# Residual block, one core: SwiGLU results, residual blocks and most mixer outputs turned into tables by DMA transposes of 16-bit halves instead of TensorE transposes

## The chip, the cores and the metric

The kernel runs on one core of one Trainium2 chip. The metric is the device time of one execution in microseconds (us), the median of several runs. TensorE (PE) multiplies, VectorE (DVE) and ScalarE (ACT) work on tiles in SBUF and PSUM, GpSimd (POOL) does little here, and SyncE (SP) issues the DMAs of the weights.

## The reference

One layer of a streaming encoder on 256 tokens of width 2048, all in fp32:

```python
proj = rmsnorm(x, g_mix) @ w_in                  # 2048 x 10240: two mixers' q, k, v and two gates
merged = sigmoid(gate_sb) * (y_sb @ w_sb_out) + sigmoid(gate_ca) * (y_ca @ w_ca_out)
x = x + merged @ w_mix_out                       # 2048 x 2048
g_ff, u_ff = split(rmsnorm(x, g_ffn) @ w_ffn_in) # 2048 x 11264
x = x + (silu(g_ff) * u_ff) @ w_ffn_out          # 5632 x 2048
x = x + sigmoid(rmsnorm(x, g_ple) @ w_ple_gate) * (p @ w_ple_in)
out = rmsnorm(x, g_final)
```

`y_sb` and `y_ca` are two attention mixers of 8 heads each. With 256 tokens, nearly all the work is the products of the 256-row activations with the weights.

## The kernel before

**Tables.** A product needs its activations with the contracted feature on the partitions. They stand in *tables*: T1 (the input, later the merged mixer output, later the input of the last gate), T2 (the mixers' outputs, later the SwiGLU results) and T3 (the input of the feed-forward). A table holds for each of up to 16 feature tiles of 128 a high part and a low part (`fp32r` splits of the fp32 value); every product is made of three fp32r matmuls, high with high, high with low, low with high (`three`, L305).

**How a table is made.** `into_table` (L473) takes a 256-token by 512-feature fp32 block (`src`). TensorE transposes it in eight 128x128 transposes into PSUM (L482). `table_part` (L489) then makes the split: ScalarE copies PSUM to the high part (L504), VectorE subtracts for the low part (L505, by `minus`, L257). Where the feature pair is one that is multiplied by a fast scheme of seven products instead of eight (a "pair"), ScalarE copies PSUM to a plain tile `af` first (L496), and `sums_of` (L462) makes four sums (`fm`) and their split (the forms FP, F_more, F_out, F_last). For a norm's input each value is scaled by the gain on the way (L508, L509). 23 blocks become tables this way: 4 of the merged mixer output (key `mg`), 4 of the residual for the feed-forward (`ffn`), 11 of SwiGLU results (`h0`, `h1`, `h2`: 3, 4 and 4 blocks) and 4 of the residual for the last gate (`ple`).

**Weights.** They are streamed. SP issues one DMA of 512 KB for each raw tile (L241) into seven places (five, and two more in the late part of the kernel); it waits until a place has been read. ScalarE casts a raw tile to its high part `hi` (L277, and L292, L295 for the two tiles of a pair piece), VectorE subtracts to make `lo` (L257). Up to four `hi` and `lo` tiles exist, and TensorE multiplies from them.

**Order.** The work is a list of *pieces*. A single piece has one raw tile and twelve 512-wide matmuls; a pair piece has two raw tiles and 21 matmuls. `flush` (L436) loops over the pieces: it loads as far as there are places, splits up to three pieces ahead, and writes out the products of the present one. Other work is a queue of tasks, one of which is run after a piece; `later` puts a table's making three tasks behind. `split` (L259) runs tasks at once when a piece needs a table that isn't made yet. A scheduler then sets the order in each engine's queue, which is executed in that order.

The feed-forward takes 3 blocks of 12, 16 and 16 feature tiles. In each, 3 or 4 units make a SwiGLU block (two 512-wide weight columns, 16 raw tiles) and put it into C; then two units multiply with `w_ffn_out`. C is one buffer with four 512-wide slots, C[:, 0] to C[:, 3]: the result stands in the first two; the last two are free after `in_post` has used them. The pieces of the first output unit of the first block come in the order 0, 0, 1, 1, -2, 3, 3, -4, 5, 5 (L40; a minus is a pair piece), and piece -4 needs the forms F_more of the last SwiGLU block of that part.

Of the kernel before, what the change touches and what calls it, by code (L numbers as in the profile page):

```python
# [8 lines left out]

F32 = mybir.dt.float32  # L10
F32R = mybir.dt.float32r
AF = mybir.ActivationFunctionType
ALU = mybir.AluOpType
AX = mybir.AxisListType
# [2 lines left out]
P = 128  # L17
S = 256
# [34 lines left out]
def block_kernel(ctx: ExitStack, tc: tile.TileContext, x, p, w_in, w_sb_out, w_ca_out, w_mix_out,  # L53
# [95 lines left out]
    pieces = []  # L149
    held = deque()  # L150
    tasks = deque()
    done = set()

    def run_task():
# [104 lines left out]
    def split(pc):  # L259
        for k in pc["needs"]:  # L260
            while k not in done:
                run_task()
        raws = pc.pop("raw")
        state["raw"] -= len(raws)
        for _ in raws:
            held.popleft()
        if pc["g"]["kind"] == "unit" and len(raws) == 2:
            return split_pair(pc, *raws)
        raw, = raws
        n = raw.shape[1]  # L270
        if pc["g"]["keep"] is None:
            hi, lo = buffers(n)
        else:
            hi, lo = (t[:, pc["kts"][0] * pc["ncol"] :][:, :n] for t in pc["g"]["keep"])
        m = n // 2 if pc is pieces[0] else n
        for c in range(0, n, m):
            state["cast"] = nc.scalar.copy(hi[:, c : c + m], raw[:, c : c + m])  # L277
# [158 lines left out]
    def flush(every=1, until=None, in_turn=False):  # L436

        n = 0
        while state["at"] < len(pieces) and (until is None or until not in done):
            pc = pieces[state["at"]]  # L440
            prefetch()
            products(pc)
            seed_next()
            state["at"] += 1
            n += 1
            if tasks and every and not state["hold"] and int(n / every) > int((n - 1) / every):
# [39 lines left out]
        for k in range(4):  # L486
            done.add((key, 4 * c + k))

    def table_part(dst, kt, ps, gain, forms, pairs):  # L489
        n = ps.shape[1]  # L490
        ks = slice(kt, kt + n)
        g = None if gain is None else [gT[:, gain + kt + k : gain + kt + k + 1] for k in range(n)]
        if forms is not None and kt // 2 in pairs:
            af = state["work"]("af").rearrange("p (k s) -> p k s", k=2)
            if g is None:
                nc.scalar.copy(af, ps)  # L496
            else:
                for k in range(2):
                    nc.scalar.activation(af[:, k, :], ps[:, k, :], AF.Identity, scale=g[k])
            nc.scalar.copy(dst[:, ks, 0, :], af)  # L500
            minus(dst[:, ks, 1, :], af, dst.bitcast(F32)[:, ks, 0, :])
            sums_of(af, forms(kt))
        elif g is None:
            nc.scalar.copy(dst[:, ks, 0, :], ps)  # L504
            minus(dst[:, ks, 1, :], ps, dst.bitcast(F32)[:, ks, 0, :])  # L505
        else:
            for k in range(n):
                nc.scalar.activation(dst[:, kt + k, 0, :], ps[:, k, :], AF.Identity, scale=g[k])  # L508
                nc.vector.scalar_tensor_tensor(dst[:, kt + k, 1, :], ps[:, k, :], g[k], dst.bitcast(F32)[:, kt + k, 0, :],  # L509
                                               ALU.mult, ALU.subtract)  # L510
# [412 lines left out]
    def out_post(m, c):  # L923
        def post(ps):
            cs = slice(c * NB, (c + 1) * NB)
            gt = gates[:, :, m, cs]
            for t in range(NT):
                by = rstd if (m, c) == (1, 0) else r1
                with tc.issue_after(state["cast"].ins):
                    nc.scalar.activation(gt[:, t, :], gt[:, t, :], AF.Sigmoid, scale=by["mix"][:, t : t + 1])  # L930
            for t in range(NT):
                nc.vector.tensor_tensor(gates[:, t, m, cs], ps[t], gates[:, t, m, cs], ALU.mult)
            if m == 1:
                mg = gates[:, :, 0, cs]
                nc.vector.tensor_tensor(mg, mg, gt, ALU.add)
                later(lambda: into_table(T1, c, mg, key="mg", forms=lambda kt: FP[:, kt // 4 - 2], pairs=MIX_PAIRS))
        return post

    for m, wo in ((0, w_sb_out), (1, w_ca_out)):
# [27 lines left out]

    def next_tables(T, c, gain, key, pool):

        for cc in (c - 1, c):  # L970
            fn = lambda cc=cc: into_table(T, cc, x_[:, :, cc * NB : (cc + 1) * NB], gain, key, pool=pool)
            if cc == c:
                tasks.append((None, fn))
# [71 lines left out]

    def hidden(dst, c, key, g, pairs):
        C = late["C"]
        later(lambda: into_table(dst, c, C[:, :2, :], key=key, pool=g["pool"],
                                 forms=out_form(pairs), pairs=pairs))

    def in_post(dst, c, key, pairs):
        def post(g, b):
# [169 lines left out]
```

## Time and profile before

| | |
|---|---|
| median of 3 runs | 1456.3 us (1455.9 to 1456.44) |
| the profiled execution's own time | 1455.66 us |
| its span in the trace | 1453.9 us |
| granted TensorE clock | 0.998 |
| busy share of the span: TensorE, VectorE, ScalarE | 99%, 86%, 57% |
| mean DMA rate | 200 GB/s |

Busy times are unions of the instructions' records, and a matmul's record (391 ns for 512 columns) is longer than the step from one matmul to the next, since they are pipelined. So what a matmul costs is read from the starts in the timeline. In a group of instructions the columns are line, engine, operation, tiles (out<-in), shapes and count, then busy us and the mean ns of one, then the idle time of the engine just before them and what ended it. SPq is SyncE's queue, which only issues.

### The profile page before, as it was taken

What the parts mean: (1) busy time and instruction counts of PE and PEld (TensorE: products, weight loads), DVE (VectorE), ACT (ScalarE), POOL (GpSimd) and SP (SyncE); (2) the same over time, 40 slices, a digit from 0 to 9 for tenths busy, and PEclk for the clock granted to TensorE, in tenths of its full rate; (3) what the DMA queues carried; (4) which work ended last, traced back from release to release, by engine and by line L of the source; (5) the groups of instructions that cost most, each with busy time, mean ns of one, the idle gap of its engine ahead of it and who ended that gap; (6) DMA issues with size and microseconds to landing.
All of it is one profiled execution on the core that took longest, in us unless ns stands there. A gap on an engine that the chain in (4) does not pass through costs nothing.

```text
span 1453.9 us, 18702 instructions
## 1 busy us (share of the span) xinstructions
PE 1443.5 (99%) x6837; PEld 1208.8 (83%) x6837; DVE 1249.7 (86%) x1587; ACT 829.6 (57%) x993; POOL 25.1 (2%) x44
## 2 busy tenths in 40 slices
PE   9999999999999999999999999999999999999997
PEld 7888888888888888888888888888888888888886
DVE  6979777898987767888999999999999989999785
ACT  6456555655545665555556655566655556666652
POOL 0200000000010000000000000000000000000100
PEclk9999999999999999999999999999999999999999
DMA  9866555666675655765666666666666666665871
GB/s 319 283 189 212 181 172 172 180 205 198 199 257 164 180 168 181 231 204 173 198 192 189 196 222 194 199 201 208 193 194 216 195 186 201 215 189 178 275 230 70
DMA packets 164731, 291.17 MB, mean 200 GB/s; under 512 B 9024, under 2 KB 42096, under 8 KB 164384
## 3 DMA queue, kind: packets, MB, share of 16 engines
q1 hardware_dynamic: 162528, 281.32, 62.0%
q0 software_dynamic: 2112, 8.68, 1.8%
q8 instruction: 53, 0.87, 0.2%
q14 instruction: 38, 0.31, 0.1%
HBM read 284.19 MB, written 5.77 MB: 199 GB/s over the span
## 4 chain that ended last, share of the span: by engine, by line
PE 96%; DVE 2%; DMA 1%; issue 1%; ACT 0%; DVEq 0%; SPq 0%; ACTq 0%
PE mm L307 67%; PE su L307 13%; PE mm L392 8%; PE mm L394 4%; PE tp L482 1%; DVE lo L257 1%; DMA raw<-in_w_in 1%; PE mml L307 0%; DMA raw<-in_w_ple_in 0%; PE mm L382 0%; PE xps L536 0%; DVE xf L257 0%; PE yp L709 0%; ACT hi L277 0%; PE wt L800 0%
## 5 line engine op out<-in xcount | busy, mean ns | idle before, releaser
L307 PE MATMUL mm<-hi,T 128*128 128x512 f32 x2650 | 854.6, 391 | 0.4 <-DVE v L854 0.4
L257 DVE TENSOR_TENSOR lo<-raw,hi 128x1024 fp32r<-128x1024 f32 (+1 forms) x517 | 625.1, 1221 | 121.9 <-ACT hi L277 113.0
L277 ACT CAST hi<-raw 128x1024 fp32r<-128x1024 f32 (+1 forms) x379 | 396.7, 1050 | 381.0 <-PE mm L307 257.8
L307 PEld LDWEIGHTS mm<-hi,T 128*128 128x128 f32 x2650 | 497.3, 188 | 103.0 <-issue 0.8
L307 PE MATMUL mm<-lo,T 128*128 128x512 f32 x1325 | 517.1, 391 | 0.0
L307 PEld LDWEIGHTS mm<-lo,T 128*128 128x128 f32 x1325 | 248.9, 188 | 50.7
L392 PE MATMUL mm<-T,hi 128*128 128x512 f32 x512 | 179.8, 398 | 0.0
L394 PE MATMUL mm<-T,lo 128*128 128x256 f32 x512 | 139.7, 280 | 0.0
L295 ACT CAST hi<-raw 128x1024 fp32r<-128x1024 f32 x69 | 72.7, 1053 | 76.2 <-DVE raw L257 29.5
L257 DVE TENSOR_TENSOR T<-xf,T 128x1536 fp32r<-128x1536 f32 x61 | 107.2, 1757 | 8.0 <-ACT T L298 7.2
L392 PEld LDWEIGHTS mm<-T,hi 128*128 128x128 f32 x512 | 94.6, 188 | 20.1
L257 DVE TENSOR_TENSOR xf<-raw 128x512 f32<-128x512 f32 x138 | 95.1, 689 | 13.2 <-DMA raw<-in_w_ffn_out 4.1
L394 PEld LDWEIGHTS mm<-T,lo 128*128 128x128 f32 x512 | 96.7, 189 | 2.3
L298 ACT CAST T<-xf 128x1536 fp32r<-128x1536 f32 x61 | 90.2, 1479 | 12.7 <-DVE xf L257 12.3
L292 ACT CAST hi<-raw 128x1024 fp32r<-128x1024 f32 x69 | 72.6, 1052 | 31.0 <-PE mm L307 20.5
L307 PE MATMUL mm<-T,T 128*128 128x512 f32 (+1 forms) x279 | 77.2, 371 | 0.0
L307 PE MATMUL su<-hi,T 128*128 128x512 f32 x170 | 66.1, 394 | 0.0
L307 PEld LDWEIGHTS mm<-T,T 128*128 128x128 f32 x279 | 49.3, 188 | 9.1
L854 DVE TENSOR_TENSOR C<-su,C 128x512 f32<-128x512 f32 x72 | 47.8, 686 | 0.4
L257 DVE TENSOR_TENSOR xf<-raw,xf 128x512 f32<-128x512 f32 x69 | 47.5, 689 | 0.5
L257 DVE TENSOR_TENSOR raw<-raw 128x512 f32<-128x512 f32 x69 | 47.5, 689 | 0.4
L307 PE MATMUL su<-T,FP 128*128 128x512 f32 x174 | 47.3, 389 | 0.0
(280 smaller groups left out, 1242.7 us busy)
## 6 DMA issues: line engine op xcount, KB each, us to landing
raw<-in_w_ffn_in SPq DMA_DIRECT2D x176, 512.0 KB, 4.1
raw<-in_w_in SPq DMA_DIRECT2D x160, 512.0 KB, 4.4
raw<-in_w_ffn_out SPq DMA_DIRECT2D x88, 512.0 KB, 4.4
raw<-in_w_mix_out SPq DMA_DIRECT2D x32, 512.0 KB, 4.6
raw<-in_w_ple_gate SPq DMA_DIRECT2D x32, 512.0 KB, 4.9
raw<-in_w_sb_out SPq DMA_DIRECT2D x16, 512.0 KB, 3.8
raw<-in_w_ca_out SPq DMA_DIRECT2D x16, 512.0 KB, 4.5
x<-in_x SPq DMA_DIRECT2D x4, 512.0 KB, 10.2
```

Source lines behind the costliest of these rows:

```text
L257: return nc.vector.tensor_tensor(out, a, b, ALU.subtract)
L277: state["cast"] = nc.scalar.copy(hi[:, c : c + m], raw[:, c : c + m])
L292: nc.scalar.copy(h1, raw1)
L295: nc.scalar.copy(h2, raw2)
L298: nc.scalar.copy(xh, xf)
L307: state["mm"] = nc.tensor.matmul(ps, u, v, start=first, stop=last, skip_group_check=True)
L392: nc.tensor.matmul(ps, hi[:, i, f], lhs[:, kt, :, :].rearrange("p c s -> p (c s)"), start=a, stop=False)
L394: nc.tensor.matmul(ps[:, :S], lo[:, i, f], lhs[:, kt, 0, :], start=False, stop=z)
L482: nc.tensor.transpose(ps[:, k, t * P : (t + 1) * P], src[:, t, (k0 + k) * P : (k0 + k + 1) * P], ident)
L854: nc.vector.tensor_tensor(C[i], q, C[j], ALU.add)
```

## The change

20 of the 23 blocks no longer pass through TensorE: all 11 SwiGLU blocks, all 4 `ffn` blocks, two of the four `ple` blocks and three of the four `mg` blocks. For each of them

- ScalarE copies the fp32 block, taken as pairs of 16-bit words, into two planes, the lower words and the upper words (L502 after the change: two copies of 128x1024 words, one for each 128 tokens);
- SP issues DMA transposes of the planes in 16-bit elements: two of 128x1024 (L506) where the destination takes both halves in one piece, or four of 128x512 (L509) for the `mg` blocks;
- ScalarE copies the transposed halves back into interleaved words, which gives the transposed fp32 values in `af` (L517: four copies of 128x512 words);
- `table_part` then reads `af` in place of PSUM, and its own copy to `af` falls away.

The planes, and the destinations of the transposes, lie in the free slots of C (for `mg` in the gates' buffer, for some residual blocks also in a new tile `turned`). These steps are no tasks; they stand in a list `asides` with the piece after which each is due: the planes and the transposes 2 pieces behind the end of the unit (4 for the second of two residual blocks), the copies back 4 and 5 pieces later.

```diff
+    def turn(src, planes, turned, whole):
+        words = src.bitcast(U16).rearrange("p t (n h) -> p t h n", h=2)
+        planes = planes.bitcast(U16).rearrange("p t (h n) -> p t h n", h=2)
+        for t in range(NT):
+            nc.scalar.copy(planes[:, t], words[:, t])
+        for t in range(NT):
+            ts = slice(t * P, (t + 1) * P)
+            if whole is not None:
+                dma_w.dma_start_transpose(whole[:, :, ts], planes[:, t].rearrange("p h n -> p (h n)"))
+            else:
+                for h in range(2):
+                    dma_w.dma_start_transpose(turned[h][:, :, ts], planes[:, t, h, :])
+    def turned_part(dst, kt, turned, k0, gain, key, forms, pairs):
+        af = state["work"]("af").rearrange("p (k s) -> p k s", k=2)
+        words = af.bitcast(U16).rearrange("p k (s h) -> p h k s", h=2)
+        with tc.issue_after(state["cast"].ins):
+            for h in range(2):
+                nc.scalar.copy(words[:, h], turned[h][:, k0 : k0 + 2, :])
+        table_part(dst, kt + k0, af, gain, forms, pairs, af)
+    def into_table_by_dma(dst, c, src, planes, rooms, key, gain=None, forms=None, pairs=PAIRS, wait=2):
...
+        at = state["at"] + wait
+        steps = [(at, lambda: turn(src, planes, turned, whole))]
+        for i in range(2):
+            steps.append((at + 4 + i, lambda i=i: turned_part(dst, 4 * c, turned, 2 * i, gain, key, forms, pairs)))
...
     def hidden(dst, c, key, g, pairs):
         C = late["C"]
-        later(lambda: into_table(dst, c, C[:, :2, :], key=key, pool=g["pool"],
-                                 forms=out_form(pairs), pairs=pairs))
+        into_table_by_dma(dst, c, C[:, :2, :], C[:, 2:, :], room_halves(C[:, :2, :]), key, forms=out_form(pairs), pairs=pairs)
```

The rows below are SP's queue in the feed-forward, first before: weight loads alone, 48 and 24 of the first block, 64 of the second.

```order
L241 DMA raw<-in_w_mix_out 128x2x512 x32
L241 DMA raw<-in_w_ffn_in 128x2x512 x48
L241 DMA raw<-in_w_ffn_out 128x2x512 x24
L241 DMA raw<-in_w_ffn_in 128x2x512 x64
L241 DMA raw<-in_w_ffn_out 128x2x512 x32
```

And after, from the end of the first block's input weights on:

```order
L244 DMA raw<-in_w_ffn_in 128x2x512 x3
L244 DMA raw<-in_w_ffn_out 128x2x512 x14
L506 DMA_TRANSPOSE C<-C 128x8x128 x2
L244 DMA raw<-in_w_ffn_out 128x2x512 x10
L244 DMA raw<-in_w_ffn_in 128x2x512 x28
L506 DMA_TRANSPOSE C<-C 128x8x128 x2
L244 DMA raw<-in_w_ffn_in 128x2x512 x16
```

Two transposes of a SwiGLU block now stand between the loads, and the loads behind them are issued after them.

The second place is ScalarE's queue at the end of the first block's third SwiGLU unit, whose table the first output unit needs soonest. Before (tp is the PSUM tile of TensorE's transposes):

```order
L1057 ACTIVATE C<-C,r_ffn 128x512
L295 CAST hi<-raw 128x1024
L277 CAST hi<-raw 128x1024 x2
L292 CAST hi<-raw 128x1024
L496 COPY af<-tp 128x512
L504 CAST T_72<-tp 128x2x256
L500 CAST T_72<-af 128x2x256
L295 CAST hi<-raw 128x1024
L298 CAST T_71<-xf 128x1536
L277 CAST hi<-raw 128x1024
L470 CAST F_more<-fm 128x512
```

And after (C<-C is a plane, af<-C is a copy back of transposed words):

```order
L283 CAST hi<-raw 128x1024
L502 COPY C<-C 128x1024
L283 CAST hi<-raw 128x1024
L502 COPY C<-C 128x1024
L298 CAST hi<-raw 128x1024
L301 CAST hi<-raw 128x1024
L283 CAST hi<-raw 128x1024
L517 COPY af<-C 128x512 x2
L304 CAST T_71<-xf 128x1536
L556 CAST T_72<-af 128x2x256
L283 CAST hi<-raw 128x1024
L478 CAST F_more<-fm 128x512
```

Between the second plane and the first copy back stand three casts of weights here (two or three in the other SwiGLU units), and the cast of F_more now stands behind one cast of weights more than before.

More of the change, by code (lines that the diff above doesn't have):

```diff
@@ L11 @@
 F32R = mybir.dt.float32r
+U16 = mybir.dt.uint16
 AF = mybir.ActivationFunctionType
@@ L151, in block_kernel @@
     tasks = deque()
+    asides = []
+    turning = set()
     done = set()
@@ L261, in split @@
             while k not in done:
-                run_task()
+                if k in turning:
+                    asides.pop(0)[1]()
+                else:
+                    run_task()
         raws = pc.pop("raw")
@@ L445, in flush @@
             n += 1
+            while asides and asides[0][0] <= state["at"]:
+                asides.pop(0)[1]()
             if tasks and every and not state["hold"] and int(n / every) > int((n - 1) / every):
@@ L487, in into_table, with word_halves, room_halves, table_part @@
             done.add((key, 4 * c + k))
-    def table_part(dst, kt, ps, gain, forms, pairs):
+    def turn(src, planes, turned, whole):
[7 more added lines that the diff above has]
+                dma_w.dma_start_transpose(whole[:, :, ts], planes[:, t].rearrange("p h n -> p (h n)"))
+            else:
+                for h in range(2):
[7 more added lines that the diff above has]
+        table_part(dst, kt + k0, af, gain, forms, pairs, af)
+        for k in range(k0, k0 + 2):
+            done.add((key, kt + k))
+    def into_table_by_dma(dst, c, src, planes, rooms, key, gain=None, forms=None, pairs=PAIRS, wait=2):
+        turned, whole = rooms
+        turning.update((key, 4 * c + k) for k in range(4))
+        at = state["at"] + wait
+        steps = [(at, lambda: turn(src, planes, turned, whole))]
+        for i in range(2):
+            steps.append((at + 4 + i, lambda i=i: turned_part(dst, 4 * c, turned, 2 * i, gain, key, forms, pairs)))
+        asides.extend(steps)
+        asides.sort(key=lambda v: v[0])
+    def word_halves(v):
+        return [u.rearrange("p (k s) -> p k s", s=S) for u in (v[:, i].bitcast(U16) for i in range(2))], None
+    def room_halves(v):
+        v = v.rearrange("p t n -> p (t n)").bitcast(U16)
+        return [u.rearrange("p (k s) -> p k s", s=S) for u in (v[:, :1024], v[:, 1024:])], v.rearrange("p (k s) -> p k s", s=S)
+    def table_part(dst, kt, ps, gain, forms, pairs, af=None):
         n = ps.shape[1]
@@ L493, in table_part @@
         if forms is not None and kt // 2 in pairs:
-            af = state["work"]("af").rearrange("p (k s) -> p k s", k=2)
-            if g is None:
+            if af is None:
+                af = state["work"]("af").rearrange("p (k s) -> p k s", k=2)
+            if af is ps:
+                pass
+            elif g is None:
                 nc.scalar.copy(af, ps)
@@ L935, in post @@
                 nc.vector.tensor_tensor(mg, mg, gt, ALU.add)
-                later(lambda: into_table(T1, c, mg, key="mg", forms=lambda kt: FP[:, kt // 4 - 2], pairs=MIX_PAIRS))
+                forms = lambda kt: FP[:, kt // 4 - 2]
+                if c < 3:
+                    into_table_by_dma(T1, c, mg, gt, word_halves(mg), "mg", forms=forms, pairs=MIX_PAIRS)
+                else:
+                    later(lambda: into_table(T1, c, mg, key="mg", forms=forms, pairs=MIX_PAIRS))
         return post
@@ L968, in next_tables @@
     def next_tables(T, c, gain, key, pool):
+        C = late["C"]
         for cc in (c - 1, c):
+            if key == "ffn" or cc < 2:
+                if cc < c:
+                    planes, room = C[:, 2:, :], late["pool"].tile([P, 2, NB], F32, tag="turned", name="turned")
+                else:
+                    planes, room = C[:, :2, :], C[:, 2:, :]
+                into_table_by_dma(T, cc, x_[:, :, cc * NB : (cc + 1) * NB], planes, room_halves(room), key, gain,
+                                  wait=2 if cc < c else 4)
+                continue
             fn = lambda cc=cc: into_table(T, cc, x_[:, :, cc * NB : (cc + 1) * NB], gain, key, pool=pool)
```

## The prediction

> **What bounds the kernel now.** The page's busy shares and its chain come first, because they tell whose time the change takes away.
>
> ```profile
> span 1453.9 us, 18702 instructions
> PE 1443.5 (99%) x6837; PEld 1208.8 (83%) x6837; DVE 1249.7 (86%) x1587; ACT 829.6 (57%) x993; POOL 25.1 (2%) x44
> PE 96%; DVE 2%; DMA 1%; issue 1%; ACT 0%; DVEq 0%; SPq 0%; ACTq 0%
> ```
>
> TensorE is busy nearly all the time and carries 96% of the chain that ended last. A busy TensorE need not be at its peak, so I look at the feed-forward, where 17 of the 20 changed tables lie, in the table of windows, and at who waits there.
>
> ```profile
> core 0: us, PE busy (x) PEld busy (x) DVE busy (x) ACT busy (x) POOL busy (x), PEclk, DMA share, GB/s
> 605.00:1365.00 760.00, 760.00 (x3430) 630.63 (x3429) 708.18 (x863) 448.84 (x508) 4.53 (x5) 1.00 0.65 200
> ACT hi L277 <- PE mm L307: 158.8, 93, 6.0
> ACT hi L277 <- DMA raw<-in_w_ffn_in: 5.3, 2, 4.6
> SPq L241 <- DVE lo L257: 914.6, 406, 7.9
> ```
>
> In these 760 us TensorE never idles, VectorE is at 93%, ScalarE at 59%, the DMA engines at 65%. ScalarE waits for TensorE to give back `hi` tiles (158.8 us), hardly for weights (5.3 us), and SP waits for a raw place, not the reverse. Whatever leaves TensorE's queue shortens the kernel, as long as its feed keeps up.
>
> **What the change removes.** Next come the transposes themselves, and TensorE's timeline around one table.
>
> ```profile
> L482 PE MATMUL tp<-ident,C x88: 270/273/277, 710.6 to 1285.3; 128*128 128x128 f32 x88
> L482 PE MATMUL tp<-ident,x x64: 270/273/277, 620.9 to 1364.9; 128*128 128x128 f32 x64
> L482 PE MATMUL tp<-ident,gates x32: 270/273/276, 542.8 to 579.0; 128*128 128x128 f32 x32
> 756.45 0.39 PE L307 MATMUL mm<-T,T 128*128 128x512 f32 x1
> 756.68 0.38 PE L482 MATMUL tp<-ident,C 128*128 128x128 f32 x2
> 756.82 0.48 PE L307 MATMUL su<-hi,T 128*128 128x512 f32 x1
> 757.13 0.82 PE L482 MATMUL tp<-ident,C 128*128 128x128 f32 x6
> 757.70 0.48 PE L307 MATMUL su<-lo,T 128*128 128x512 f32 x1
> 758.02 0.40 PE L307 MATMUL su<-hi,T 128*128 128x512 f32 x1
> 758.25 0.40 PE L307 MATMUL mm<-lo,T 128*128 128x512 f32 x1
> ```
>
> There are 88 + 64 + 32 = 184 transposes, eight for each of 23 tables. A transpose is recorded with 273 ns, but that isn't what it costs. From 756.68 to 758.02, 1.34 us, TensorE started eight transposes and two matmuls; a matmul's step is 0.23 us (756.45 to 756.68), so the eight cost 1.34 - 0.46 = 0.88 us. The change takes 20 tables away: 20 x 0.88 = 17.6 us. This is the whole gain that it can have, since TensorE hardly idles for anything that the transposes cause; it would be 43.7 us by the records, which overlap.
>
> **What it adds on ScalarE.** The trace has no copy of 16-bit words. The nearest rows are the casts and copies of the same counts.
>
> ```profile
> L277 ACT CAST hi<-raw 128x1024 fp32r<-128x1024 f32 x185 | 193.9, 1053 | 192.0 <-PE mm L307 158.8 <-issue 12.8 <-PE su L307 10.1
> L496 ACT COPY af<-tp 128x512 f32<-128x512 f32 x11 | 6.4, 584 | 2.2 <-PE tp L482 2.2
> ```
>
> A table takes two planes of 1024 (2 x 1.05 us) and four copies back of 512 (4 x 0.58 us): 4.4 us. For 17 tables in the feed-forward that is 75 us, less the 11 copies to `af` that fall away (6.4 us): ScalarE goes from 449 to about 518 us of some 745, 70%. I take these durations; half of them, were 16-bit words faster, or twice, were strided words slower, would leave it at 64% and 80%. The first row shows what hides this: 192 us in which ScalarE idles before a weight cast. Without that cover the 4.4 us would delay the casts, and TensorE, by up to that much for each table. VectorE's instructions stay the same in number and size (the subtractions read SBUF in place of PSUM), so 708 us must now fit into 745: 95%, with 37 us left over 17 tables, about 2 us for each.
>
> **What it adds on SP and the DMA queues.** 34 transposes of 256 KB and 12 of 128 KB, 10.2 MB beside the 291 MB that move now, go into the queue that carries the weights. How long a transpose takes no row shows. The nearest are plain transfers of like sizes.
>
> ```profile
> raw<-in_w_ffn_in SPq DMA_DIRECT2D x176, 512.0 KB, 4.1
> x<-in_x SPq DMA_DIRECT2D x4, 512.0 KB, 10.2
> out<-x SPq DMA_DIRECT2D x8, 256.0 KB, 2.9
> ```
>
> A table's two transposes together are one weight tile in bytes. I call T the time from the end of the second plane to the landing of both. It lies between 2.9 us (one 256 KB store) and 20.4 us (both in series, each as slow as the slowest row); I take 5 us, near the 4.1 us of the 512 KB loads that share the queue. Behind a transpose wait the loads. A raw place is used again after seven tiles of 12 x 0.227 us, 19 us (an estimate); less 4.1 us for landing and about 2.3 us for cast and subtraction, a tile lies some 12 us before it is read. So SP may stand still for T = 5 us for nothing.
>
> The Trainium skill speaks against the change here: the page "VectorE: DVE Perf Modes", section "The three transpose paths", gives 1309 ns for a 128x128 transpose of 16-bit elements by DMA against 390 ns on TensorE, and its rules prefer TensorE where the result may go to PSUM. By its figures a table of 16 such 16-bit blocks would take 20.9 us one after another, an estimate that no run here shows yet; the trace disagrees with its other figure, 0.11 us a transpose by the starts above.
>
> **Where the wait goes.** Behind the second plane ScalarE has two or three weight casts, then the first copy back, which waits for T. The first block's third unit is the tightest place, so I read it engine by engine.
>
> ```profile
> 794.91 1.41 DVE L1059 SCALAR_TENSOR_TENSOR C<-C,r_ffn 128x512 f32<-128x512 f32 x2
> 796.12 1.06 ACT L277 CAST hi<-raw 128x1024 fp32r<-128x1024 f32 x1 [0.48 <-PE mm L307]
> 798.84 1.06 ACT L277 CAST hi<-raw 128x1024 fp32r<-128x1024 f32 x1 [1.66 <-PE mm L307]
> 800.89 1.05 ACT L292 CAST hi<-raw 128x1024 fp32r<-128x1024 f32 x1 [1.00 <-PE su L307]
> 801.91 0.59 ACT L496 COPY af<-tp 128x512 f32<-128x512 f32 x1
> 805.91 1.06 ACT L277 CAST hi<-raw 128x1024 fp32r<-128x1024 f32 x1
> 809.67 0.69 DVE L257 TENSOR_TENSOR F_more<-fm,F_more 128x512 fp32r<-128x512 f32 x1
> 811.15 0.39 PE L307 MATMUL mm<-hi,F_more 128*128 128x512 f32 x1
> ```
>
> Casts of single tiles come 2.72 us apart (796.12, 798.84), as TensorE releases tiles. Two of them cover about 5.4 us of T; beyond that ScalarE stands, and with it the casts behind, until the roughly three split pieces ahead of TensorE are used up, another 8 us. So I cost T = 5 us at nothing in the steady state, and TensorE starves for T above about 13 us.
>
> The table of the first block's third unit has no such reserve. Its source is done at 796.32, `af` is copied at 801.91, the form F_more is complete at 810.36 and TensorE first uses it at 811.15: 0.8 us to spare. After the change two planes end near 801, and three casts stand ahead of the copy back, which starts near 807 (the cast of 805.91 and its 1.06 us), whether T is 3 or 6. That is 5 us later than 801.91. With the 0.8 us of reserve TensorE waits 4.3 us there, once. It can be 0, if the shorter rest of the chain makes it up, and about 19 us for T at its upper end (801 + 20.4 against 801.91 + 0.8). The 16-tile blocks read their last table three pieces later, so nothing there.
>
> **The sum.** -17.6 + 4.3 = -13.3 us. The profiled execution took 1455.66 us, so 1442.4; the median is 0.6 us above it: 1443.0 us.
>
> **The rivals.** *The whole gain*: no wait in the first block either, 1456.3 - 17.6 = 1438.7 us; I count it with the forecast.
>
> *The feed becomes the bound.* VectorE's 2 us left for each table also pay for its waits behind ScalarE. If ScalarE's bursts of 4.4 us cost it 0.5 us of TensorE a table, 10 us of the gain are lost: 1453 us; if all 0.88 us, it is no change, 1456. For it speaks VectorE's 93%; against it, that ScalarE now waits for TensorE 158.8 us and not the reverse.
>
> *Slow transposes hold ScalarE's queue: slower.* Place: the first copy back of each table. It costs from T of about 13 us on, where the first block's wait, 801 + T against 802.7, is 11 us already; with 0.33 us more for each of 20 tables, T = 13.3, the 17.6 us are gone, and from there it is slower. At T = 20.4 us each of the 20 tables costs 20.4 - 13 = 7.4 us, 148 in all, and the first block 11 more: 1456.3 - 17.6 + 148 + 11 = 1598 us. At T = 14.5 it is 1456.3 - 17.6 + 30 + 11 = 1480 us. For it: a transpose moves 16-bit elements, and no row shows one. Against it: the bytes are those of one load of 4.1 us, and the DMA engines have 35% left. By the figure of the Trainium skill quoted above ("VectorE: DVE Perf Modes", "The three transpose paths") T would be 20.9 us, this case.
>
> **The chances.** About 0.2%, 2.9 us, is what a measurement of this kernel can tell from no change: faster is below 1453.4, slower above 1459.2. The forecast with the whole gain (1438 to 1448): 0.55. A feed that eats part of it (1448 to 1453.4): 0.14. All of it eaten (to 1459.2): 0.06. Slow transposes: 0.25, of which 0.06 up to 1465 and 0.19 beyond. So faster 0.69, same 0.06, slower 0.25. From 1438 to 1465 lie 0.55 + 0.14 + 0.06 + 0.06 = 0.81; the forecast's own range is 1438 to 1448.
>
> **What would show it.** Right: 24 transposes left on TensorE; no step over 0.23 us between matmuls at the changed tables but for some 4 us before the first F_more matmul of the first output unit; transposes landing within 5 us; ScalarE near 518 us in the feed-forward; loads still not waited for. Wrong: transposes landing after more than 10 us, copies back (L517) that wait for them, weight casts late behind these, and TensorE waiting for `hi` or `lo` in every unit; or VectorE idle behind ScalarE with TensorE waiting for `lo`.

## The result, and the profile after

The changed kernel takes 1473.45 us (median of 4 runs, 1471.65 to 1476.47) beside 1456.1 us of the kernel before (1455.57 to 1456.44): ratio 1.012, 95% interval 1.0108 to 1.0132. It is 17.4 us slower; the forecast was 13.3 us faster, its own range ended at 1448 us, and the wider one at 1465. The profiled execution took 1473.71 us.

The page of the kernel after, the lines that answer to those of before: span, busy shares, and the chain by engine.

```profile
span 1472.0 us, 18564 instructions
PE 1437.7 (98%) x6677; PEld 1193.7 (81%) x6677; DVE 1249.6 (85%) x1587; ACT 905.9 (62%) x1101; POOL 23.7 (2%) x44
PE 81%; DVE 6%; DMA 5%; ACT 4%; issue 3%; SPq 1%; DVEq 0%; ACTq 0%
```

TensorE has 160 instructions less, and carries 81% of the chain instead of 96%: the chain now runs over other engines for a fifth of the span. The table of windows for the feed-forward, and then the waits of TensorE, the longest groups, say how much it stands still.

```profile
605.00:1365.00 760.00, 739.14 (x3215) 605.48 (x3213) 691.36 (x843) 501.15 (x580) 1.31 (x2) 0.99 0.69 206
```

```profile
PE mm L313 <- ACT T L564: 7.5, 1, 7.5
PE su L313 <- ACT T L556: 5.2, 1, 5.2
PE mm L313 <- ACT hi L301: 2.7, 3, 1.6
PE mm L313 <- DVE lo L260: 2.1, 3, 1.4
PE mm L313 <- DVE T L565: 2.1, 1, 2.1
PE mm L313 <- ACT hi L283: 1.4, 4, 0.6
```

TensorE was busy for all 760 us of that window, and is now for 739. Three waits make up 14.8 us of it: they are waits for a table (`T`, cast by L564 or L556, its low part by L565), and each happens once. Where the time goes is seen when the matmuls into the PSUM tiles `mm` and `su`, in which the products are summed, are counted from the start in both traces. Transposes are not among them, so a number means about the same point of the work in both; the times are in us:

```
matmul   starts before   after    after - before
 2500        555.0       553.4        -1.6
 3000        673.9       673.6        -0.3
 3100        697.0       711.1       +14.1
 3400        766.9       779.1       +12.2
 3600        813.2       831.5       +18.3
 4600       1043.6      1058.2       +14.6
 4700       1066.2      1082.2       +15.9
 5500       1250.3      1264.3       +14.0
 5950       1355.1      1373.0       +18.0
```

Between the losses the change gains 0.9 us for every table, as reckoned. It loses some 6 us ahead of matmul 3000, where seven tables should have gained 6.3 us and only 0.3 are left. It loses 14.4 us in the first unit of the feed-forward (matmuls 3000 to 3100), some 7 us at the first output unit (before 3600, a table's gain included), and smaller amounts at the output units of the second and third part (4700, 5950). In the first feed-forward unit, ScalarE's timeline:

```profile
677.71 1.40 ACT L517 COPY af<-turned 128x512 uint16<-128x512 uint16 x2 [1.55 <-DMA turned<-C]
678.98 1.04 ACT L283 CAST hi<-raw 128x1024 fp32r<-128x1024 f32 x1
679.92 0.90 ACT L564 ACTIVATE T<-af,gT 128x256 fp32r<-128x256 f32 x2
680.73 1.04 ACT L283 CAST hi<-raw 128x1024 fp32r<-128x1024 f32 x1
689.84 1.99 ACT L283 CAST hi<-raw 128x1024 fp32r<-128x1024 f32 x2 [8.07 <-PE mm L313]
694.23 0.62 ACT L478 CAST FP<-fm 128x512 fp32r<-128x512 f32 x1 [2.40 <-DVE fm L260]
694.75 1.38 ACT L517 COPY af<-turned 128x512 uint16<-128x512 uint16 x2
696.00 1.36 ACT L517 COPY af<-C 128x512 uint16<-128x512 uint16 x2
697.24 1.70 ACT L564 ACTIVATE T<-af,gT 128x256 fp32r<-128x256 f32 x4
```

The transposed words of the two residual blocks had landed at 677.61 and 682.16. Yet the copies back come at 694.75, because two casts of weights and the cast of FP stand ahead of them in ScalarE's queue. The casts of weights wait 8.07 us for TensorE to give back an `hi` tile; TensorE, which wants the table, does so only as it creeps on. The cast of FP then waits 2.40 us for VectorE's sums. TensorE's side of the same stretch, and the granted clock in the windows around it and around the first output unit:

```profile
682.21 0.40 PE L313 MATMUL mm<-lo,T 128*128 128x512 f32 x1
684.73 0.97 PE L313 MATMUL mm<-hi,T 128*128 128x512 f32 x3 [2.12 <-DVE T L565]
...
688.73 0.61 PE L313 MATMUL mm<-lo,T 128*128 128x512 f32 x1
689.16 1.10 PE L313 MATMUL mm<-hi,T 128*128 128x512 f32 x4
697.78 0.79 PE L313 MATMUL mm<-hi,T 128*128 128x512 f32 x1 [7.52 <-ACT T L564]
698.37 0.63 PE L313 MATMUL mm<-lo,T 128*128 128x512 f32 x1
698.80 0.63 PE L313 MATMUL mm<-hi,T 128*128 128x512 f32 x1
```

```profile
685.80:689.20 3.40, 3.40 (x10) 2.66 (x9) 2.82 (x4) 0.00 (x0) 0.00 (x0) 0.50 0.74 264
692.60:702.80 10.20, 5.02 (x12) 3.95 (x13) 6.50 (x15) 6.93 (x14) 0.00 (x0) 0.50 0.33 103
825.70:829.10 3.40, 2.95 (x7) 2.37 (x8) 3.40 (x4) 2.96 (x5) 0.00 (x0) 0.50 0.84 324
```

After each wait the clock is granted at 0.50 for 3.4 or 10.2 us, and the step between matmuls is 0.43 us (698.37 to 698.80) instead of 0.23. In the first unit that makes 2.1 + 7.5 us of waits and 22 matmuls of 0.2 us more, 14.0 of the 14.4 us; at the first output unit 5.2 us and 7 x 0.2 us, 6.6 of about 7. The page "TensorE: Matmul & The Clock Gate" of the Trainium skill, part 1, gives such a window 3413 ns and the half rate after an idle one; the trace agrees with the length, but here a wait of 2.1 us was already followed by such a window.

The transposes themselves, from the view of their line, and the copies on ScalarE from the groups by shape:

```profile
L506 SPq DMA_TRANSPOSE C<-C x28: 1232/1296/3728, 633.1 to 1347.5; - x28
DMA to landing us min/median/max: 2.7/3.8/6.7
```

```profile
L517 ACT COPY af<-C 128x512 uint16<-128x512 uint16 x56 | 38.9, 767 | 21.9 <-DMA C<-C 18.2 <-DVE T L565 3.2 <-DVE T L260 0.4
L502 ACT COPY C<-C 128x1024 uint16<-128x1024 uint16 x22 | 22.3, 1042 | 1.9 <-DVE C L1127 1.9
```

A transpose of 256 KB lands 3.8 us after its issue, and from the end of the second plane to the last landing (T) it takes 4.1 to 8.0 us for the eleven SwiGLU tables, median 5.3. So the transposes are in the median what was forecast. At the first output unit, where two loads were issued just ahead, T was 8.0 us; SP's queue there, and the copy back that waits for the landing:

```profile
813.67 1.50 SPq L244 DMA_DIRECT2D raw<-in_w_ffn_out  x2
815.23 5.46 SPq L506 DMA_TRANSPOSE C<-C  x2
822.87 1.38 ACT L517 COPY af<-C 128x512 uint16<-128x512 uint16 x2 [3.09 <-DMA C<-C]
```

The planes took 1.04 us as reckoned, a copy back 0.77 us instead of 0.58; but two in a row overlap and take 1.38 us (694.75 above).

### The profile page after: what moved, and what is told of

Read it like the earlier page. It is cut to its first block, busy times and chain, and to the rows that moved or that the text cites. A ratio compares the mean times of both kernels' runs of the same rounds, so it can differ in the third digit from the quotient of the medians.

```text
span 1472.0 us, 18564 instructions
## 1 busy us (share of the span) xinstructions
PE 1437.7 (98%) x6677; PEld 1193.7 (81%) x6677; DVE 1249.6 (85%) x1587; ACT 905.9 (62%) x1101; POOL 23.7 (2%) x44
## 4 chain that ended last, share of the span: by engine, by line
PE 81%; DVE 6%; DMA 5%; ACT 4%; issue 3%; SPq 1%; DVEq 0%; ACTq 0%
PE mm L313 56%; PE su L313 10%; PE mm L398 8%; PE mm L400 4%; DVE lo L260 3%; DMA C<-C 2%; ACT af L517 1%; ACT hi L283 1%; DVE xf L260 1%; DMA raw<-in_w_ffn_out 1%; DMA raw<-in_w_ffn_in 1%; DMA raw<-in_w_mix_out 1%; DMA raw<-in_w_ple_in 1%; DMA raw<-in_w_in 1%; DVE T L260 1%
## 5 line engine op out<-in xcount | busy, mean ns | idle before, releaser
L260 DVE TENSOR_TENSOR lo<-raw,hi 128x1024 fp32r<-128x1024 f32 (+1 forms) x517 | 623.2, 1217 | 105.8 <-ACT hi L283 96.4
L517 ACT COPY af<-C 128x512 uint16<-128x512 uint16 x56 | 38.9, 767 | 21.9 <-DMA C<-C 18.2
## 6 DMA issues: line engine op xcount, KB each, us to landing
x<-in_x SPq DMA_DIRECT2D x4, 512.0 KB, 10.3
```

What stands on the lines that cost most here:

```text
L260: return nc.vector.tensor_tensor(out, a, b, ALU.subtract)
L517: nc.scalar.copy(words[:, h], turned[h][:, k0 : k0 + 2, :])
```

## The experiments

Four theories were tried. **Q**, queue order: the copies back stand in ScalarE's queue behind casts that wait for TensorE, which costs only where a table is due soon. **T**: the transposes, by their time, SP's queue or their landings, cost something for each table. **F**: ScalarE's added work delays the casts of weights everywhere. **V**, which came up later: VectorE, with the same work in less time, has no room left. The scheduler sets the queues of every variant anew, so that their order can also differ at places that an edit doesn't name.

### The two late tables

**Feed-forward tables back on TensorE** (four of the 20 blocks):

```diff
-            if key == "ffn" or cc < 2:
+            if key != "ffn" and cc < 2:
```

> The four residual blocks of the feed-forward's input go through TensorE again; the other 16 tables stay as after the change (1473.45 us). Theory Q (queue order: the loss sits at the two or three places where a table is due soon, since its copies back stand in ScalarE's queue behind weight casts that wait for TensorE; elsewhere a table gains 0.9 us): the first feed-forward unit lost 14.4 us against before and the stretch ahead of it some 2.5 us, and four tables cost 3.7 us again: about 1460 us. Theory T (the transposes themselves: their landing and the loads behind them cost about the same for every table, 0.87 us net each): 1470 us.

Measured: 1458.59 us, ratio 1.0018 (1.0009 to 1.0027). 15 us of the loss hang on these four tables, although each gives up its gain of 0.9 us. That is Q's figure. TensorE's wait at the first output unit stays (4.4 us, with T = 8.2 us).

**Feed-forward tables copied back earlier**: all 20 still by DMA, but for the key `ffn` both parts are copied back 2 pieces after the transposes instead of 4 and 5, and the planes of the second block stand 3 pieces behind its unit instead of 4.

```diff
-            steps.append((at + 4 + i, lambda i=i: turned_part(...)))
+            steps.append((at + (gap + i if gap == 4 else gap), lambda i=i: turned_part(...)))
-                                  wait=2 if cc < c else 4)
+                                  wait=2 if cc < c else (3 if key == "ffn" else 4), gap=2 if key == "ffn" else 4)
```

> All 20 tables stay on DMA transposes; for the four residual blocks the copies back are due 2 pieces behind the transposes in place of 4 and 5, and the second block's planes 3 pieces behind the unit in place of 4, so that ScalarE's queue has about five fewer weight casts ahead of the last copies back. The transposes are the same. Theory Q: TensorE's wait of 7.7 us in the first feed-forward unit and part of its other 6 us go: 1461 to 1467 us. Theory T: nothing lands sooner, so 1472 to 1475 us.

Measured: 1457.83 us, ratio 1.0011 (1.0002 to 1.0021). The same transposes, issued and copied back a few pieces earlier, are worth 15.6 us, more than Q said. By the count of matmuls 12.6 us of it come back in the first feed-forward unit. The rest comes mainly from the first output unit, which the edit doesn't touch: there the transposes were issued with only one load just ahead, T was 4.6 us instead of 8.0, and one cast of weights instead of three stood ahead of the copy back. TensorE's longest waits for a table, from the view of the waits of this kernel:

```profile
PE mm L313 <- ACT T L564: 1.6, 1, 1.6
PE su L313 <- ACT T L556: 1.5, 1, 1.5
```

The 7.5 us and 5.2 us are down to 1.6 and 1.5, and the clock stays full (granted at 1.00 from 680 to 700 us).

**The last SwiGLU table of the first part back on TensorE**, the one that the first output unit needs soonest:

```diff
+        if (key, c) == ("h0", 2):
+            later(lambda: into_table(dst, c, C[:, :2, :], key=key, pool=g["pool"], forms=out_form(pairs), pairs=pairs))
+            return
```

> Only the last SwiGLU block of the first part goes through TensorE again. Theory Q: the first output unit's loss of 7.0 us against before goes, one table costs 0.9 us again: 1467 us. Theory T: one table of 20: 1472.6 us.

Measured: 1469.15 us, ratio 1.0092 (1.0076 to 1.0108). The wait of 5.2 us is gone; 4.3 of some 7 us came back (2 to 6 by the interval), between Q's 1467 and T's 1472.6.

**Without the transposes, at the places of the change.** The copies back read the planes instead of transposed words, so nothing is transposed. ScalarE's order stays much the same in the first feed-forward unit; at the first output unit the scheduler put one cast of weights instead of three ahead of the copy back.

```diff
-                dma_w.dma_start_transpose(whole[:, :, ts], planes[:, t].rearrange("p h n -> p (h n)"))
...
-                nc.scalar.copy(words[:, h], turned[h][:, k0 : k0 + 2, :])
+                nc.scalar.copy(words[:, h], rooms_of[id(turned)][:, k0 // 2, h, :].rearrange("p (k s) -> p k s", k=2))
```

> The whole change with only the DMA transposes left out (copies back read the planes, at the places in ScalarE's queue where the change has them). Q in its pure form (the copies are late because of what stands ahead of them in the queue, not because of the transposes): the late table of the first feed-forward unit stays, 1466 to 1474. T (lateness comes from landings): 1440 to 1456.

Measured: 1462.73 us, ratio 1.0045 (1.003 to 1.0061): between the two. ScalarE's timeline and TensorE's longest wait in this kernel (its L513 and L560 are L517 and L564 above):

```profile
684.39 1.99 ACT L283 CAST hi<-raw 128x1024 fp32r<-128x1024 f32 x2 [4.17 <-PE mm L313]
690.91 0.62 ACT L478 CAST FP<-fm 128x512 fp32r<-128x512 f32 x1 [4.53 <-DVE fm L260]
691.44 2.61 ACT L513 COPY af<-C 128x512 uint16<-128x512 uint16 x4
693.92 1.69 ACT L560 ACTIVATE T<-af,gT 128x256 fp32r<-128x256 f32 x4
```

```profile
PE mm L313 <- ACT T L560: 9.7, 1, 9.7
```

With no transfer to wait for, TensorE still waits 9.7 us, for a copy that stands behind casts: in the first unit Q holds in its pure form, though 4.53 us of ScalarE's idle time there are a wait for VectorE's sums. The wait at the first output unit is absent, but with two casts fewer ahead of the copy this run does not part queue and landing there. The trace of the change does: the casts ahead of the copy back were done at 819.79, and it waited 3.09 us more for the landing (T = 8.0 us). So some 3 of the 5.2 us are the landing's, and some 2 are left for the queue. Where the landing held the copy for 2.26 us (the four feed-forward tables on TensorE, T = 8.2) TensorE waited 4.4 us, and for 3.72 us (eleven SwiGLU tables, below, T = 9.4) 5.9: about 2 us more each time.

**The copies back on GpSimd.** The whole change, and the variant with early copies, with one call changed:

```diff
-                nc.scalar.copy(words[:, h], turned[h][:, k0 : k0 + 2, :])
+                nc.gpsimd.tensor_copy(words[:, h], turned[h][:, k0 : k0 + 2, :])
```

> The whole change, with only the 80 copies back (L517) moved from ScalarE to GpSimd, which is idle 98% of the span. They no longer stand behind weight casts, and no weight cast stands behind them; ScalarE keeps the planes, 2.1 us a table. Queue order (Q): the late tables of the first feed-forward unit and the first output unit come in time, 1473.5 - 14 - 7 = about 1453 (1450 to 1458, as when the copies were issued earlier). ScalarE's work as well (F): 61 us less on ScalarE, of which 0.4 of each us cost TensorE when copies were doubled, so another 10 us or more below that: 1440 to 1448. Transposes (T): the copies still wait for the same transposes, so near 1470. If GpSimd's copies are much slower than ScalarE's 0.77 us, or slow VectorE beside them, above 1473.

> As the variant whose feed-forward tables are copied back early (1457.8), with the 80 copies back on GpSimd. Q: little is left for it to gain, 1454 to 1458. F: 61 us of ScalarE's work gone, so 10 us or more lower, 1440 to 1448. T: unchanged, 1457 to 1460.

Measured: 1473.68 us, ratio 1.0121 (1.0107 to 1.0134), and 1473.99 us, ratio 1.0122 (1.0109 to 1.0136). What Q and F said did not come in either kernel, and the second even lost 16 us to its partner; for the first, the caution on slow GpSimd copies (above 1473) came true. ScalarE's timeline of the first of the two shows one reason:

```profile
686.42 1.99 ACT L283 CAST hi<-raw 128x1024 fp32r<-128x1024 f32 x2 [4.02 <-PE mm L313]
691.57 0.62 ACT L478 CAST FP<-fm 128x512 fp32r<-128x512 f32 x1 [3.17 <-DVE fm L260]
693.59 0.91 ACT L564 ACTIVATE T<-af,gT 128x256 fp32r<-128x256 f32 x2 [1.40 <-POOL af L517]
```

The cast into the table (L564) is still ScalarE's, behind the same casts of weights, and TensorE still waits 7.3 us for it: the copies had left the queue, the table's cast had not. The groups show the other reason, GpSimd's copies and VectorE's subtractions in the kernel with early copies:

```profile
L260 DVE TENSOR_TENSOR lo<-raw,hi 128x1024 fp32r<-128x1024 f32 (+1 forms) x517 | 636.4, 1242 | 107.7 <-ACT hi L283 99.6
L517 POOL COPY af<-C 128x512 uint16<-128x512 uint16 x56 | 91.1, 1674 | 560.6 <-DMA C<-C 299.3
```

A copy takes 1.67 us in the mean instead of 0.77, and VectorE's `lo` 1242 ns instead of 1217: VectorE is busy 1273.9 us for the same 1587 instructions that took 1248.1. So these runs say little of F; they replaced ScalarE's load by one on VectorE.

### What is left without the late tables

**Ten SwiGLU tables only**: `mg`, `ffn`, `ple` and, by the lines shown for it above, the last block of the first part stay on TensorE.

```diff
-                if c < 3:
+                if False:
...
-            if key == "ffn" or cc < 2:
+            if False:
```

> Only ten SwiGLU blocks use DMA transposes: all but the last one of the first part. The mixer outputs and all residual blocks go through TensorE. Theory Q: 1456.1 - 10 x 0.9 = 1447 us, faster than both kernels. Theory T: 1456.1 + 10 x 0.87 = 1465 us.

Measured: 1454.34 us, ratio 0.999 (0.9981 to 0.9999). No wait of TensorE for a table or a cast behind one is longer than 0.4 us in the feed-forward, and still only 1.8 of 8.8 us are left, between Q's 1447 and T's 1465. By the count of matmuls each table gains its 0.9 us, and the ends of the three parts, at their output units, give 2.4, 1.0 and 3.6 us back.

**The same with every transpose issued twice**, the second time into a tile that nobody reads:

```diff
+                dma_w.dma_start_transpose(room_halves(spare)[1][:, :, ts], planes[:, t].rearrange("p h n -> p (h n)"))
```

> Ten SwiGLU blocks by DMA (that kernel took 1454.3 us), and each of their 20 transposes is followed by a second one of the same plane into a tile that nobody reads; ScalarE's and TensorE's work is unchanged. Theory T (the transposes' own time on SP and the DMA queue is what costs): the cost of ten tables doubles, 9 us more: 1463 us. Theory Q (queue order) and theory F (ScalarE's added work delays the weight casts): within 2 us of 1454.3.

Measured: 1458.55 us, ratio 1.002 (1.001 to 1.0029), 4.2 us more for ten tables. A second pair of transposes costs 0.4 us a table, half of what T said, and more than the 2 us in all that Q and F allowed.

**The same with every copy back made twice** (40 more copies):

```diff
+                nc.scalar.copy(words[:, h], turned[h][:, k0 : k0 + 2, :])
```

> The same ten blocks, with each of the 40 copies back done twice, one behind the other: 40 more copies on ScalarE with a step of about 0.62 us, 25 us in all, at the same places of its queue. Theory F: TensorE loses half of it or more, 1466 us and up. Theory Q: ScalarE idles long enough behind the copies; only the table that is due soonest comes later: within 4 us of 1454.3. Theory T: no change.

Measured: 1464.59 us, ratio 1.0057 (1.0043 to 1.0071), 10.3 us more. ScalarE's busy time rose by 24 us (865.5 to 889.5; copies in a row overlap, two take 1.38 us), so 0.4 of each added us reaches TensorE, though ScalarE is busy for only 61% of the span. Q, by which a copy off the tight places costs nothing, falls here; F's 1466 was missed by 1.4 us.

**All 20 tables with early copies, ten and eleven SwiGLU tables with early copies, eight SwiGLU tables.** The first three set the distance to 2 pieces for all tables (all 20; the 11 SwiGLU tables; the ten of above); the last leaves the last block of each part on TensorE. In the first three the default of `gap` becomes 2 as well.

```diff
-                                  wait=2 if cc < c else (3 if key == "ffn" else 4), gap=2 if key == "ffn" else 4)
+                                  wait=2 if cc < c else 3)
...
-        if (key, c) == ("h0", 2):
+        if (key, c) in (("h0", 2), ("h1", 3), ("h2", 3)):
```

> All 20 tables by DMA as after the change, but for every one the copies back are due 2 pieces behind the transposes in place of 4 and 5 (with the residual blocks alone so, 1457.8 us were measured). Theory Q: the first output unit's wait (4.7 us of loss left there) shrinks too: 1452 to 1456 us. Theories T and F: no further gain, 1458 us.

Measured: 1458.99 us, ratio 1.0018 (1.0009 to 1.0027); earlier copies of the other tables bring nothing, as T and F said.

> All eleven SwiGLU blocks by DMA with the earlier copies back, mixer outputs and residual blocks on TensorE. Theory Q: eleven gains of 0.9 us, less the losses of the output units, which were 7 us with the late copies back and should be some 4: 1449 to 1452 us, the fastest so far. Theory F: as with ten blocks or slower, 1454 us.

Measured: 1459.52 us, ratio 1.0021 (1.0013 to 1.003). The first part's last table is late by 5.9 us again, even when copied back early, since its transposes land late (T = 9.4 us, again behind two loads).

> Eight tables by DMA: those of the SwiGLU blocks that are not the last of their part; the last block of each of the three parts, whose table the first output unit needs soonest, stays on TensorE with all others. Q with due times: each of the eight gains 0.88 us and nothing is due soon, 1456.1 - 7 = 1449 (1448 to 1451). F: every table pays ScalarE's 5.2 us wherever it lies, as the ten did (1454.3, 0.17 us a table), so about 1454.7 (1453.5 to 1456). T: 0.4 us of each table's gain is lost to the transposes, 1452.

Measured: 1454.36 us, ratio 0.9984 (0.9975 to 0.9993). The tables that are due soonest cost no more than the others here: Q's 1449 failed, F's 1454.7 came, and what eats the gain is not bound to a late table.

> The ten SwiGLU tables by DMA (1454.3), each copied back two weight tiles after its planes instead of four and five. Q: earlier copies spare the output units, 1450 to 1453. F and T: the copies cost the same wherever they stand and now wait longer for the landings, 1454 to 1458.

Measured: 1453.03 us, ratio 0.9977 (0.9968 to 0.9986). Among the kernels that compute the layer it is the only one that beats both by more than 0.2%: 3.2 us under the kernel before, and 20 under the change. From the ten tables with late copies (1454.3) the intervals do not part it, so Q's earlier copies are not shown to help.

**Ten SwiGLU tables, copies on GpSimd** (the edit of above):

> The ten SwiGLU tables by DMA (1454.3 with copies on ScalarE), with the 40 copies back on GpSimd. F: 31 us less on ScalarE; doubling the same copies cost 10.3 us, so taking them away gains up to what is lacking to the whole gain of 8.8 us: 1447 to 1450. Q: the copies hold nobody now, 1448 to 1452 (the waits of 12 us for transposes leave ScalarE's queue). T: the transposes remain, 1453 to 1455.

Measured: 1458.4 us, ratio 1.0011 (1.0002 to 1.002), 4 us worse, and above what any of the three said; VectorE's busy time rose from 1248.6 to 1262.9 us.

### Taking the added work away

These start from the 20 tables with early copies (1457.8 us), where no table is late by more than 1.6 us.

**Nothing added**: no planes, transposes or copies back; the casts read the untransposed block, which is handed over as `turned`.

```diff
-        steps = [(at, lambda: turn(src, planes, turned, whole))]
+        steps = []
...
-        af = state["work"]("af").rearrange("p (k s) -> p k s", k=2)
+        af = turned[:, k0 // 2, :].rearrange("p (k s) -> p k s", k=2)
```

> All 20 tables, due as in the variant with early feed-forward copies (1457.8), but with planes, transposes and copies back left out: the casts and subtractions read the untransposed source, so this leaves the transposition out of the computation. TensorE, VectorE and the casts do what they do in that variant; ScalarE has even less work than before. If ScalarE's added work (F) or the transposes and their waits (T, Q) took the gain, the whole of it appears: 1438 to 1441. If the limit is VectorE (V), whose work stays the same in less time and which is 95 to 100% busy where the output units lose, little changes: 1450 to 1456.

Measured: 1444.89 us, ratio 0.9922 (0.9909 to 0.9936). Neither: 11.2 of the 17.6 us. The window of the feed-forward in this kernel:

```profile
605.00:1365.00 760.00, 757.79 (x3332) 622.58 (x3332) 714.86 (x872) 445.88 (x505) 3.48 (x5) 1.00 0.65 204
```

VectorE has 94% there, and TensorE has holes again. By the count of matmuls the 6.2 us are lost at the output units of the three parts (1.1, 1.5 and 3.6 us), the places where the ten tables lost theirs. The last of them, in the kernel before and in this one:

```profile
1310.00:1345.00 35.00, 35.00 (x164) 29.17 (x163) 33.78 (x43) 23.14 (x35) 0.09 (x1) 1.00 0.57 174
1310.00:1345.00 35.00, 33.44 (x138) 24.86 (x137) 32.72 (x37) 21.06 (x26) 0.58 (x1) 1.00 0.63 207
```

VectorE's mean of 93% before was 97% in this stretch. With nothing added it is 93% here, while TensorE starts 26 matmuls fewer; that VectorE is the reason is shown only by the two runs on its share below.

**Planes and copies back, no transposes** (the edit of the kernel without transposes, on the early variant):

> The same variant with planes and copies back kept on ScalarE (5.2 us a table) and only the DMA transposes left out: the copies back read the planes, so the blocks are not transposed. F (ScalarE's work takes the gain): near 1457.8, 1455 to 1459. T and Q (the transposes, SP's queue, waits for landings take it): 1440 to 1446. V: 1450 to 1456, as with nothing added.

Measured: 1454.27 us, ratio 0.9988 (0.998 to 0.9997). ScalarE's planes and copies cost 9.4 us for 85 us of its busy time (821.7 to 906.5), 4.2 us a table; with the transposes added the variant stands at 1457.8, 3.6 us more (about 1 to 6 by the two intervals). What T and Q said here (1440 to 1446) did not come; the time lies in V's range and just below F's.

**VectorE's share.** On the kernel with nothing added, the subtraction for the low part of the 20 tables is made twice, or is replaced by a copy on ScalarE:

```diff
             minus(dst[:, ks, 1, :], ps, dst.bitcast(F32)[:, ks, 0, :])
+            if af is ps:
+                minus(dst[:, ks, 1, :], ps, dst.bitcast(F32)[:, ks, 0, :])
```

```diff
-            minus(dst[:, ks, 1, :], ps, dst.bitcast(F32)[:, ks, 0, :])
+            if af is ps:
+                nc.scalar.copy(dst[:, ks, 1, :], ps)
```

> The variant with nothing added (1444.9, the transposition left out), with VectorE's subtraction for the low part of each of the 20 tables made twice: 28 instructions of 0.69 us and 24 of about 0.4 us, some 28 us of VectorE's work more. If VectorE is what holds that variant 6 us above the whole gain of 1438.7 (V), it loses at least as much per us as ScalarE did when its copies were doubled (0.4): 1456 or more. If VectorE still has room: 1445 to 1449.

Measured: 1454.04 us, ratio 0.9986 (0.9977 to 0.9995): 9.2 us more for 22 us of VectorE's busy time (1250.9 to 1273.0), 0.4 us for each. V's 1456 had been reckoned with 28 us. TensorE's largest waits there are for `lo` of the weights (2.8 us), not for the tables.

> The variant with nothing added, with the low part of the 20 tables written by a ScalarE copy in place of VectorE's subtraction: about 28 us less on VectorE and 25 to 30 us more on ScalarE; the low parts then hold the high parts' values, so the split is left out for these tables too. V: the 6 us come back, 1438.5 to 1441. If it is ScalarE that holds the variant: 1447 or more. Neither, about 1445: what is left is order, not work.

Measured: 1437.39 us, ratio 0.9873 (0.9859 to 0.9886). The 6 us come back, and one more. The page and the same window of this kernel:

```profile
PE 1424.1 (99%) x6677; PEld 1191.2 (83%) x6677; DVE 1224.9 (85%) x1535; ACT 841.9 (59%) x1033; POOL 23.8 (2%) x44
```

```profile
605.00:1365.00 760.00, 760.00 (x3363) 629.66 (x3362) 695.49 (x830) 468.10 (x555) 3.47 (x5) 1.00 0.65 205
```

ScalarE has 20 us more than with nothing added (821.7) and TensorE has no hole left: VectorE's subtractions were the limit, and V is shown for this part. This run alone does not part their time from their place behind the high part's cast, which a copy need not wait for; that doubled subtractions delay `lo` speaks for the time.

## Why the prediction was wrong

From the whole gain, 1438.7 us, to the measured 1473.5 us are 34.8 us. The runs, each the one before with something added, divide them:

```
the whole gain (reckoned)                              1438.7
VectorE, with its work unchanged   nothing added       1444.9    +6.2
planes and copies back on ScalarE  no transposes       1454.3    +9.4
the transposes                     early copies        1457.8    +3.6
the change's own places            the change          1473.5   +15.6
```

The shares depend on the order of the steps: the places of the change cost 8.4 us without transposes (1462.7 against 1454.3) and 15.6 with them (2 to 3 of these at the first output unit, which the edit doesn't move), and the transposes cost 3.6 us with early copies but 10.8 at the places of the change (1473.5 against 1462.7).

- **The gain of 0.88 us a table** was right: 0.90 to 0.95 between the losses.
- **"The first block's third unit is the tightest place"** is the step that failed most. It looked only at SwiGLU tables. The four residual tables of the feed-forward, which the first feed-forward unit reads at once, were not looked at. Copied back 4 and 5 pieces behind the transposes, they came after casts that wait for TensorE: 14 us, of which 4.4 us are the half clock. That T was about 5 us did not help; in the first unit the queue made the wait, not the transfer (9.7 us without any transfer).
- **The 4.3 us reckoned for that third unit** came near the measured 5.2 us in part by luck. The sum had the copy back late by the three casts ahead of it, whether T is 3 or 6, and no wait for the landing. Some 2 us are left for the casts; the other 3.1 us are the landing, since T was 8.0 us where the sum took 5. The 1.4 us of half clock after the wait were not in the sum.
- **ScalarE's work hidden by 192 us of idle time** failed as well. Its size was right (4.2 us a table against 4.4), its cost was not nothing but 9.4 us, 0.1 of each us; the next 24 us, when copies were doubled, cost 0.4 of each. The idle time before the casts is a wait for an `hi` tile, so it is not free at every moment when a copy is due.
- **VectorE at 95%, "37 us left"**, was the third error: the number was right, that it suffices was not. It is a mean, and at the output units of the last part VectorE had 97% before. With nothing added at all, 6.2 us are lost there and at the other output units. The rival "the feed becomes the bound" had mechanism and size (0.5 to 0.88 us a table, 1453 to 1456 us): the two feed terms make 15.6 us over 20 tables, 0.78 each, and the kernel without transposes took 1454.3. It got a chance of 0.20, which was too little beside that 93%.
- **Transposes at nothing below T = 13 us** was nearly right away from the tight place: T was 5.3 us in the median, and with early copies the whole term is 3.6 us, 0.2 us a table (0.4 when doubled). At the first output unit T = 8.0 us added 3.1 us of waiting. The rival "slow transposes" gave the right sign; its landing above 13 us did not occur, and a late landing cost much in that one table alone. By the 1309 ns a block of the page "VectorE: DVE Perf Modes" of the Trainium skill, section "The three transpose paths", the eight blocks of one transpose would take 10.5 us in series, an estimate; here they landed in 2.7 to 6.7 us.

What stays open: how much of ScalarE's 9.4 us would be left if VectorE had room, since the casts that the copies delay reach TensorE through VectorE's subtractions. No run has both the copies and a relieved VectorE.

## What to carry to other kernels

Where an instruction's result is due, and what stands ahead of it in its engine's queue, has to be looked up for every place that the change touches, the first unit of the next stage above all: here the late tables of one unit cost 14 us, most of the 17.6 us that 20 tables could gain, and 4.4 us of it only because the clock was halved after the waits. A mean busy share of 93% on an engine that feeds the bound engine hid stretches of 97%, and there it became the next bound here; of work that is put on it, or on its supplier, expect part of each us to be lost (here 0.1 to 0.4), whatever its mean idle time says. Moving a small step to an idle engine helps only if no consumer of it stays in the old queue, and if the idle engine doesn't slow the busy one.

## What the runs showed of the hardware

- GpSimd beside VectorE: GpSimd's copy of 128x512 16-bit words took 0.75 us at its fastest and up to 7.4 us (in the whole change with its copies there), and VectorE's total rose by 26 us at the same instructions (the variant with early copies). The page "GPSIMD Engine Reference" of the Trainium skill, section "Specifications", says that the two share SBUF interfaces and contend where VectorE has two SBUF inputs; the subtraction `lo<-raw,hi` has two, and the trace agrees (1217 to 1242 ns in the mean).
- A wait of 2.1 us was enough for a stretch of 3.4 us at half clock, and one of 7.5 us for 10.2 us. In the variant with early copies waits of 1.6 us were followed by none, but in the kernel with the last SwiGLU table of the first part on TensorE one of 1.39 us (to 594.80) was followed by 3.4 us at 0.50 (597.0 to 600.4). So the length of the wait alone does not decide it.
- ScalarE's copy of 512 16-bit words into every second word took 767 ns, a copy of 512 fp32 values 584 ns; 1024 words into dense planes took 1042 ns, about as much as an fp32 cast of that count (1053 ns).
- SP was held 1.3 us in the median by the issue of a transpose of 128x1024 words, and 3.7 us by the one at the first output unit, with two loads just ahead, against 0.37 us for most weight loads.
